# A macaron decoder block on one core: later work for the second half of a normalisation, and two overwritten 192-column products

## The chip, the cores and the metric

The kernel runs on one core of one Trainium2 chip. The metric is the device time of one execution in microseconds (us). Three runs of the kernel before took 958.99, 968.86 and 957.89 us; the median is 958.99 us. One further execution was recorded by the hardware profiler: it took 969.29 us, of which its instructions span 967.5 us.

## The reference

One decoder block on 512 tokens of width 1024: a SwiGLU feed-forward (hidden width 2816), a token mixer, a second SwiGLU feed-forward, each behind an RMSNorm with a learned shift and scale from a condition vector, and a last RMSNorm. All inputs are float32.

```python
cond = jax.nn.silu(c)
mod = cond @ w_ada[l] + b_ada[l]                      # nine vectors: shift, scale, gate, three times
u = modulate(rmsnorm(h, g_norm_ffn1[l]), sh1, sc1)
h = h + 0.5 * gt1 * swiglu(u, w_ffn1_in[l], w_ffn1_out[l])
u = modulate(rmsnorm(h, g_norm_mix[l]), sh2, sc2)
h = h + gt2 * token_mixing(u, cos, sin, ...)          # pooling and dilated attention, gated, then w_out
u = modulate(rmsnorm(h, g_norm_ffn2[l]), sh3, sc3)
h = h + 0.5 * gt3 * swiglu(u, w_ffn2_in[l], w_ffn2_out[l])
return rmsnorm(h, g_final)
def swiglu(u, w_in, w_out):
    a, b = jnp.split(u @ w_in, 2, axis=-1)
    return (jax.nn.silu(a) * b) @ w_out
```

## The kernel before, in words

**Data.** Features lie on the 128 partitions and the 512 tokens along the free axis, so the residual stream `H` is eight tiles of 128 x 512. To keep float32 accuracy every operand of a product is split in two parts, a rounded one and the rest: weights into `whi` and `wlo`, the normed input into `UH` and `UL`. One product then is three matmuls, high by high, high by low and low by high (`mm3`, lines 424 to 426; in the double pairs lines 794 to 796).

**Weights.** They come by DMA in chunks of 128 x 1024 into a few raw buffers. For each chunk ScalarE writes the rounded part (`split_hi`, line 377) and VectorE the rest (`split_lo`, line 389) into two rings, `whi` and `wlo`. The calls `look(n)` and `split(n)` in the code say how many chunks ahead of TensorE this is done. `self.half` holds a chunk whose high part is written and whose low part isn't. The order of the instructions on each engine is that in which the code calls them (a manual schedule), and each engine works through its own list; semaphores join them.

**Double pairs.** Most of the feed-forward is computed two hidden tiles at a time by a scheme of the Strassen kind, with seven products of 24 matmuls (128 x 256 each) where eight would be needed (`duo` and `product`). For that it uses sums of blocks of the input: `S[0]`, `S[1]` and `S[2]` in tiles `SH` and `SL`, made by `u_steps` (steps called `x22`, `x21`, `x11`, `x12` for the sums on VectorE, `s0`, `s1`, `s2`, `s3` for their two parts: `s0[0]` the high one on ScalarE, `s0[1]` the low one on VectorE, lines 757 and 758). The tile `X` holds four blocks, a11, a12, a21 and a22. Some of the sums of weight chunks are made on VectorE too (`X` <- raw, line 312). The output parts (`out_blocks`) use the same scheme on the hidden values.

**Around the change.** Only the way into the second feed-forward is touched. Its stages, with the times of the profiled execution:

- `out_tail` (to about 629 us) ends the mixer: the last three tiles of its output product for token half A (tokens 0 to 255), then for half B. For each tile, `tail_step` adds the product to `H` (line 600, VectorE) and squares it (line 601, ScalarE); the squares are summed into `AR` (line 651, VectorE). In half B's second tile, `stats_t` sums A's squares over the features (line 512), ScalarE takes the root (line 514), VectorE the reciprocal (line 517), and `spread` spreads it over the partitions on TensorE (line 522).
- `head` (about 629 to 650 us) computes the first two hidden pairs with whole products. In half A (loop value `h` 0) the normed input of B is begun: per tile, line 535 on VectorE, line 547 on ScalarE (`UH`), line 565 on VectorE (`UL`). Line 552 on ScalarE writes the unsplit input into `X`; for half A's upper four tiles that is put off in the list `self.rows`.
- `ffn2` then makes the sums, takes the SiLU of the first pairs (line 725) and goes into the first double pair (hidden tiles 2 and 3), at about 650 us, the second (tiles 4 and 5) and the first output part.

**Overwritten products.** `settle` (line 430) issues one matmul of 240 columns into a bank that the next product overwrites: `start=True` follows, so its result is never used. Before the change it stands at nine places in the trace, all of them ahead of 609 us.

Of the kernel before, what the change touches and what calls it, by code (L numbers as in the profile page):

```python
# [11 lines left out]
AF = mybir.ActivationFunctionType  # L12
# [4 lines left out]
HT = 256  # L17
# [121 lines left out]
SHIFT = 16  # L139

PLAIN = {0: 6, 2: 2}
# [24 lines left out]
class Kernel:  # L166
# [258 lines left out]
        M(ps, hi, ul, start=False, stop=False)  # L425
        M(ps, lo, uh, start=False, stop=stop)  # L426

    def settle(self, bank, hi, uh):

        self.nc.tensor.matmul(bank[:, :HT - SHIFT], hi, uh[:, SHIFT:HT], start=True, stop=True, skip_group_check=True)  # L430

    def nb(self):
        b = self.banks[self.bi % len(self.banks)]
# [163 lines left out]
    def tail_step(self, m, hs, bank, gate, s):  # L597

        Hm = self.H[m][:, hs]
        self.nc.vector.scalar_tensor_tensor(Hm, bank[:, hs], gate[:, m:m + 1], Hm, op0=OP.mult, op1=OP.add)  # L600
        self.nc.scalar.activation(s, Hm, AF.Square)

    def out_tail(self, ms, ksrc, gate, nxt, squares, beside=None):


        nc = self.nc
        tiles, starts, put, rest = {}, {}, [], self.spare()
        A, Bh = slice(0, HT), slice(HT, T)
        step = None
        self.held = self.pos  # L610
        for h, hs in enumerate((A, Bh)):
            for m in ms:
                bank = self.nb()
                if h == 0:
                    starts[m] = self.pos
                    tiles[m] = ksrc(m)
                    starts[m + 1] = self.pos
                if h == 0 and m == ms[0]:
                    nc.scalar.preload_act_table(AF.Sqrt)
                behind = h == 1 and m == ms[1]  # L620
                if self.done < self.pos + 4 and not behind:
                    self.split_hi()
                ks = tiles[m]
                if h == 0 and m == ms[0]:
                    self.settle(bank, ks[0][0], ks[0][2])
                for i, (hi, lo, uh, ul) in enumerate(ks):
                    if behind and i == len(ks) // 2:
                        self.stats_t(rest[0], A)
                        if self.done < self.pos + 4:
                            self.split_hi()  # L630
                        if self.half and len(self.half[1]) > 1:
                            self.split_lo(True)
                    if h == 1 and m == ms[2] and i == 0:
                        self.spread(rest[0], A)
                        step = self.norm_steps(nxt, A)
                        if nxt == 2:
                            step.three()
                        step(0)
                        self.split_lo()
                        self.fetch()  # L640
                    self.mm3(bank[:, hs], hi, lo, uh[:, hs], ul[:, hs], i == 0, i == len(ks) - 1)
                if step and m == ms[-1]:
                    step.low()
                    step.high()
                s = squares(m)[:, :HT]
                self.tail_step(m, hs, bank, gate, s)
                if h == 1:
                    self.held = starts[m + 1]
                    if step:
                        step(1 if m != ms[-1] else 3)  # L650
                put.append(lambda s=s, hs=hs: nc.vector.tensor_tensor(self.acc[:, hs], self.acc[:, hs], s, op=OP.add))
                do = lambda: [put.pop(0)() for _ in range(len(put))]
                if nxt == 2 and h == 0 and m == ms[-1]:
                    do()
                if not behind:
                    self.split_lo()
                    self.fetch()
                if beside and h == 0 and m == ms[0]:
                    beside()
                if h == 0 or m != ms[1]:  # L660
                    do()
        self.stepA = step

    def head(self, n, banks, table, between=(), beside={}):
# [9 lines left out]
        for h, hs in enumerate((A, Bh)):  # L674
            for i, (k, which) in enumerate(steps if h == 0 else [(k, both) for k in range(KT)]):
                if h == 0:
                    if i == 4:
                        self.stats_t(self.spare()[1], Bh)
                        nc.scalar.preload_act_table(table)
                    stepA(min(i, 5) + 2)  # L680
                    if i == 8:
                        self.spread(self.spare()[1], Bh)
                    if i > 7:
                        stepB(i - 8)
                        if n == 2 and i == 8:
                            stepB.low()
                            while self.rows:
                                self.rows.pop(0)()
                else:
                    stepB(k + 3)  # L690
                for f in beside.get((h, i), ()):
                    f()
                for j in which:
                    self.mm3(banks[j][:, hs], *w[j][k], self.UH[k][:, hs], self.UL[k][:, hs], k == 0, k == KT - 1)
                if (h, i) in ((0, 8), (1, 2), (1, 5)):
                    if h and between:
                        between.pop(0)()
                    if n == 2 and (h, i) == (1, 2):
                        stepB.high()
                        stepB.low()  # L700
                    self.split(self.done)
                    self.fetch()
        for f in between:
            f()
        self.held = None
# [79 lines left out]
    def product(self, bank, u, start, extra=0, other=None):  # L785
        M = self.nc.tensor.matmul
        w = self.take()
        if extra:
            self.settle(other if other is not None else bank, w[0][0], self.UH[0])
        for p in range(2):  # L790
            o = bank[:, p * HT:(p + 1) * HT]
            for k in range(4):
# [6 lines left out]
    def duo(self, n, j, first, last, extra):  # L799
# [33 lines left out]
        for i, (bank, u, start) in enumerate(((A, blk(lo4, T1), True), (B, S[0], True), (A, S[1], False),  # L833
# [10 lines left out]
                    f()  # L844
            elif not late:
                self.look(i if last and n and i > 4 else 2 if second and behind else 3 if early and i < 4 or behind or second else 4)
            w = self.product(bank, u, start, 0 if i else extra)
            if beside and i == 0:
                nc.tensor.matmul(C[:, :HT], w[0][0], u[0][0], start=False, stop=True, skip_group_check=True)
            self.step()  # L850
# [278 lines left out]
    def out_blocks(self, n, k0):  # L1129
# [72 lines left out]
    def ffn2(self):  # L1202
# [8 lines left out]
        for f in (x22, s0[0], x21):  # L1211
            f()
        h0, h1 = (self.ffn_silu(j, bk[2 * j]) for j in range(2))
        for f in (x11, s1[0], s0[1], s1[1]):
            f()
        late = self.block_hidden(0)
        two = lambda: self.look(2)
        b4, b5 = (self.banks[(self.bi + i) % 6] for i in range(2))

        def begin():  # L1220
            two()
            x12()
            s2[0]()
            self.free += self.rawx[1:]
# [1073 lines left out]
```

## Time and profile before

| | |
|---|---|
| median of 3 runs (each) | 958.99 us (958.99, 968.86, 957.89) |
| profiled execution, its span | 969.29 us, 967.5 us |
| TensorE matmuls, busy | 7352, 959.3 us (99%) |
| TensorE weight loads, busy | 907.7 us (94%) |
| VectorE busy | 842.2 us (87%) |
| ScalarE busy | 545.4 us (56%) |
| GpSimd busy | 90.5 us (9%) |
| granted TensorE clock | 0.999 |

Busy time is the union of an engine's instructions. Matmuls overlap in the record (each of 256 columns is shown with some 0.28 us while one starts every 0.113 to 0.118 us), so the start-to-start step of neighbouring matmuls says more than their duration. An instruction's idle time stands in brackets behind it in the timeline, with what ended it. A timeline row merges neighbours of one form and starts with the time from the span's start and the time that it covers.

### The profile page before, as it was taken

The numbers are of one execution on the slowest core, as the hardware profiler recorded it, in microseconds if no ns is written. First come the engines' busy times: TensorE is split into PE (matmuls) and PEld (weight loads), VectorE is DVE, ScalarE is ACT, GpSimd is POOL, SyncE is SP. The second block draws the span as 40 slices with busy tenths as digits, with TensorE's granted clock in tenths as the row PEclk, the third lists the DMA queues.
The fourth block names the chain that finished last, engine by engine and source line by source line (L and its number), as shares of the span: only waits on it lengthen the run. The fifth ranks groups of instructions, "written<-read, shape, count | busy, mean of one in ns | idle before, by whom it ended". The sixth has DMA issues, their size and how long they took to land.

```text
span 967.5 us, 18319 instructions
## 1 busy us (share of the span) xinstructions
PE 959.3 (99%) x7352; PEld 907.7 (94%) x7352; DVE 842.2 (87%) x1241; ACT 545.4 (56%) x829; POOL 90.5 (9%) x110
## 2 busy tenths in 40 slices
PE   9999999999999999999999999999999999999997
PEld 7888999999999999788899998999999999999997
DVE  7989999899998788886979768989998988879886
ACT  6453666665745453454565552477755656556555
POOL 0000100100010003007200000011011001000002
PEclk9999999999999999999999999999999999999999
DMA  9856776776868548857365446646766566665632
GB/s 357 283 191 240 209 218 166 207 207 152 223 170 246 174 153 254 260 189 197 77 186 158 137 144 224 206 102 185 200 166 161 140 173 164 166 153 140 163 81 88
DMA packets 55304, 176.81 MB, mean 183 GB/s; under 512 B 7857, under 2 KB 11569, under 8 KB 54962
## 3 DMA queue, kind: packets, MB, share of 16 engines
q1 hardware_dynamic: 44800, 141.82, 44.6%
q0 software_dynamic: 9840, 33.30, 19.2%
q8 instruction: 57, 0.93, 0.4%
q10 hardware_dynamic: 578, 0.53, 0.2%
q14 instruction: 29, 0.24, 0.1%
HBM read 135.36 MB, written 2.24 MB: 142 GB/s over the span
## 4 chain that ended last, share of the span: by engine, by line
PE 90%; DVE 4%; DMA 2%; ACT 1%; issue 1%; POOL 0%; SPq 0%; POOLq 0%; DVEq 0%; ACTq 0%
PE bank L795 15%; PE bank L794 15%; PE bank L796 15%; PE bank L424 6%; PE bank L425 6%; PE bank L426 6%; PE bank L1176 5%; PE bank L1175 5%; PE bank L1177 5%; PE bank L2219 2%; PE bank L2222 2%; PE bank L2224 1%; DVE wlo L389 1%; DMA v<-wada 1%; PE bank L1862 1%
## 5 line engine op out<-in xcount | busy, mean ns | idle before, releaser
L389 DVE TENSOR_TENSOR wlo<-raw,whi 128x1024 fp32r<-128x1024 f32 (+3 forms) x148 | 164.9, 1123 | 37.7 <-ACT whi L377 37.5
L794 PE MATMUL bank<-UH,whi 128*128 128x256 f32 x704 | 195.9, 278 | 0.0
L796 PE MATMUL bank<-UH,wlo 128*128 128x256 f32 x704 | 195.9, 278 | 0.0
L795 PE MATMUL bank<-UL,whi 128*128 128x256 f32 x704 | 195.9, 278 | 0.0
L389 DVE TENSOR_TENSOR wlo<-X,whi 128x1024 fp32r<-128x1024 f32 (+3 forms) x138 | 147.0, 1077 | 25.5 <-ACT whi L377 25.4
L377 ACT ACTIVATE whi<-raw 128x1024 fp32r<-128x1024 f32 (+3 forms) x148 | 141.3, 968 | 22.9 <-DMA raw<-wf1o 6.4
L377 ACT ACTIVATE whi<-X 128x1024 fp32r<-128x1024 f32 (+3 forms) x138 | 127.2, 942 | 42.9 <-DVE X L312 39.1
L794 PEld LDWEIGHTS bank<-UH,whi 128*128 128x128 f32 x704 | 133.5, 190 | 0.2
L795 PEld LDWEIGHTS bank<-UL,whi 128*128 128x128 f32 x704 | 132.2, 188 | 0.0
L796 PEld LDWEIGHTS bank<-UH,wlo 128*128 128x128 f32 x704 | 132.2, 188 | 0.0
L795 PE MATMUL bank<-SL,whi 128*128 128x256 f32 x432 | 120.5, 279 | 0.0
L796 PE MATMUL bank<-SH,wlo 128*128 128x256 f32 x432 | 120.4, 279 | 0.0
L794 PE MATMUL bank<-SH,whi 128*128 128x256 f32 x432 | 120.4, 279 | 0.0
L794 PEld LDWEIGHTS bank<-SH,whi 128*128 128x128 f32 x432 | 82.1, 190 | 0.0
L795 PEld LDWEIGHTS bank<-SL,whi 128*128 128x128 f32 x432 | 81.1, 188 | 0.2 <-DVE SL L758 0.2
L796 PEld LDWEIGHTS bank<-SH,wlo 128*128 128x128 f32 x432 | 81.1, 188 | 0.0
L424 PE MATMUL bank<-UH,whi 128*128 128x256 f32 (+1 forms) x240 | 80.4, 335 | 0.0
L425 PE MATMUL bank<-UL,whi 128*128 128x256 f32 (+1 forms) x240 | 79.2, 330 | 0.1
L426 PE MATMUL bank<-UH,wlo 128*128 128x256 f32 (+1 forms) x240 | 79.1, 330 | 0.0
L802 ACT ACTIVATE ev<-bank 128x512 f32<-128x512 f32 x54 | 32.1, 595 | 54.0 <-PE bank L796 53.8
L1175 PE MATMUL bank<-HI,whi 128*128 128x256 f32 x224 | 62.5, 279 | 0.0
L1176 PE MATMUL bank<-HK,whi 128*128 128x256 f32 x224 | 62.5, 279 | 0.0
(411 smaller groups left out, 2423.7 us busy)
## 6 DMA issues: line engine op xcount, KB each, us to landing
raw<-wmix SPq DMA_DIRECT2D x44, 512.0 KB, 4.2
raw<-wf1i SPq DMA_DIRECT2D x32, 512.0 KB, 5.7
raw<-wf2i SPq DMA_DIRECT2D x29, 512.0 KB, 4.5
ada<-wada SPq DMA_DIRECT2D x24, 512.0 KB, 6.0
X<-raw POOLq DMA_DIRECT2D x24, 512.0 KB, 5.2
xs<-wada SPq DMA_DIRECT2D x17, 512.0 KB, 6.0
X<-wf2i SPq DMA_DIRECT2D x15, 512.0 KB, 4.5
X<-wf1i SPq DMA_DIRECT2D x11, 512.0 KB, 4.3
```

Of the source, the lines that this page charges most:

```text
L377: self.nc.scalar.activation(self.hi[:, y], r[:, x], AF.Copy)
L389: self.nc.vector.tensor_tensor(self.lo[:, y], r[:, x], self.hi[:, y], op=OP.subtract)
L424: M(ps, hi, uh, start=start, stop=False)
L425: M(ps, hi, ul, start=False, stop=False)
L426: M(ps, lo, uh, start=False, stop=stop)
L794: M(o, hi, uh, start=start and p == 0 and k == 0, stop=False, skip_group_check=True)
L795: M(o, hi, ul, start=False, stop=False, skip_group_check=True)
L796: M(o, lo, uh, start=False, stop=k == 3, skip_group_check=True)
L802: copy = lambda o, x, f=1.0: nc.scalar.activation(o, x, AF.Copy, scale=f)
L1175: M(o, hi, uh, start=start and m % 2 == 0 and k == 0, stop=False, skip_group_check=True)
L1176: M(o, hi, ul, start=False, stop=False, skip_group_check=True)
L1177: M(o, lo, uh, start=False, stop=k == 1, skip_group_check=True)
```

## The change

1. In `out_tail`, the square of half B's first tile is issued later, behind the root of A's statistics; the sum of squares that uses it moves as well.
2. In `head`, the put-off rows (line 552, upper tiles of half A) are issued one split later, behind the high part of the next weight chunk; in half B, one split is opened up so that the last tile's `UL` stands ahead of the chunk's low part.
3. In `ffn2`, the low part of `S[0]` is issued ahead of the sum a11, the high part of the next weight chunk ahead of the high part of `S[1]`; a `look(2)` moves accordingly.
4. Two `settle` products of 192 columns are added: ahead of the second double pair of the second feed-forward, and ahead of its first output part. Each is one more weight load and one more matmul on TensorE (7050 rows become 7052).

```diff
-    def settle(self, bank, hi, uh):
+    def settle(self, bank, hi, uh, shift=SHIFT):
-        self.nc.tensor.matmul(bank[:, :HT - SHIFT], hi, uh[:, SHIFT:HT], start=True, stop=True, skip_group_check=True)
+        self.nc.tensor.matmul(bank[:, :HT - shift], hi, uh[:, shift:HT], start=True, stop=True, skip_group_check=True)
...
-        self.nc.scalar.activation(s, Hm, AF.Square)
+        return lambda: self.nc.scalar.activation(s, Hm, AF.Square)
...
                         self.stats_t(rest[0], A)
+                        while squared:
+                            squared.pop(0)()
                         if self.done < self.pos + 4:
                             self.split_hi()
                         if self.half and len(self.half[1]) > 1:
                             self.split_lo(True)
+                        do()
...
-                self.tail_step(m, hs, bank, gate, s)
+                square = self.tail_step(m, hs, bank, gate, s)
+                first = nxt == 2 and h == 1 and m == ms[0]
+                if first:
+                    squared.append(square)
+                else:
+                    square()
...
-                if h == 0 or m != ms[1]:
+                if h == 0 or m != ms[1] and not first:
                     do()
...
                             stepB.low()
-                            while self.rows:
-                                self.rows.pop(0)()
...
                         stepB.high()
                         stepB.low()
-                    self.split(self.done)
+                        self.split_lo()
+                        self.split_hi()
+                        stepB(6)
+                        stepB.low()
+                    self.split(self.done - bool(self.half))
                     self.fetch()
+                    while self.rows:
+                        self.rows.pop(0)()
...
-            self.settle(other if other is not None else bank, w[0][0], self.UH[0])
+            self.settle(other if other is not None else bank, w[0][0], self.UH[0], extra * SHIFT)
...
-            w = self.product(bank, u, start, 0 if i else extra)
+            w = self.product(bank, u, start, 0 if i else 4 if n and j == PLAIN[n] + 2 else extra)
...
             w, uk = self.take(), blk(u)
+            if n and k0 == 0 and i == 0:
+                self.settle(A[0], w[0][0], self.UH[0], 4 * SHIFT)
...
-        for f in (x11, s1[0], s0[1], s1[1]):
+        two = lambda: self.look(2)
+        for f in (s0[1], x11, two, s1[0], s1[1]):
             f()
         late = self.block_hidden(0)
-        two = lambda: self.look(2)
...
         def begin():
-            two()
             x12()
             s2[0]()
```

ScalarE at the end of the mixer's tail, half B: `gc` and `gs` are the buffers of the squares (line 601), `r_80` holds the root of A's statistics. Before:

```order
L601 ACTIVATE gs<-H 128x256
L377 ACTIVATE whi<-raw_64 128x1024
L601 ACTIVATE gc<-H 128x256 x2
L514 ACTIVATE r_80<-bank_96,eps 128x2
L377 ACTIVATE whi<-raw_65 128x512 x2
L601 ACTIVATE gs<-H 128x256
```

After:

```order
L601 ACTIVATE gs<-H 128x256
L377 ACTIVATE whi<-raw_64 128x1024
L601 ACTIVATE gc<-H 128x256
L514 ACTIVATE r_80<-bank_96,eps 128x2
L601 ACTIVATE gc<-H 128x256
L377 ACTIVATE whi<-raw_65 128x512 x2
L601 ACTIVATE gs<-H 128x256
```

The second of the two squares into `gc`, that of half B's first tile, now stands behind the root. On VectorE the reciprocal of the root moves with it, from behind the sum of that square to ahead of it.

ScalarE in `head`, at the turn from half A to half B: `UH<-ev,mod` is the high part of the normed input, `X<-ev,mod` the unsplit rows. Before:

```order
L679 ACT_TABLE_LOAD
L547 ACTIVATE UH<-ev,mod 128x256 x2
L552 ACTIVATE X<-ev,mod 128x256
L547 ACTIVATE UH<-ev,mod 128x256
L552 ACTIVATE X<-ev,mod 128x256 x4
L377 ACTIVATE whi<-raw_63 128x1024
L547 ACTIVATE UH<-ev,mod 128x256
```

After:

```order
L687 ACT_TABLE_LOAD
L547 ACTIVATE UH<-ev,mod 128x256 x2
L552 ACTIVATE X<-ev,mod 128x256
L547 ACTIVATE UH<-ev,mod 128x256
L552 ACTIVATE X<-ev,mod 128x256
L377 ACTIVATE whi<-raw_63 128x1024
L552 ACTIVATE X<-ev,mod 128x256 x3
L547 ACTIVATE UH<-ev,mod 128x256
```

Three of the four rows have moved behind the high part of the chunk `raw_63`, and ahead of the next `UH`.

VectorE between `head` and the first double pair: `X_6245` and `X_6246` are weight chunks, the plain `X` the blocks of the input, `SL_6251` and `SL_6253` the low parts of `S[0]` and `S[1]`. Before:

```order
L312 TENSOR_TENSOR X_6246<-raw_65,X_6245 128x1024
L389 TENSOR_TENSOR wlo<-X_6245,whi 128x1024
L565 SCALAR_TENSOR_TENSOR UL<-ev,mod,UH 128x256
L753 TENSOR_TENSOR X<-X 128x1024 x2
L762 SCALAR_TENSOR_TENSOR X<-X 128x1024
L758 TENSOR_TENSOR SL_6251<-X,SH_6250 128x1024
L758 TENSOR_TENSOR SL_6253<-X,SH_6252 128x1024
L389 TENSOR_TENSOR wlo<-X_6246,whi 128x1024
L762 SCALAR_TENSOR_TENSOR X<-X 128x1024
```

After:

```order
L312 TENSOR_TENSOR X_6246<-raw_65,X_6245 128x1024
L565 SCALAR_TENSOR_TENSOR UL<-ev,mod,UH 128x256
L389 TENSOR_TENSOR wlo<-X_6245,whi 128x1024
L765 TENSOR_TENSOR X<-X 128x1024 x2
L770 TENSOR_TENSOR SL_6251<-X,SH_6250 128x1024
L774 SCALAR_TENSOR_TENSOR X<-X 128x1024
L389 TENSOR_TENSOR wlo<-X_6246,whi 128x1024
L770 TENSOR_TENSOR SL_6253<-X,SH_6252 128x1024
L774 SCALAR_TENSOR_TENSOR X<-X 128x1024
```

`UL` of the last tile has moved ahead of a low part, `SL_6251` ahead of the sum a11, and the low part of `X_6246` ahead of `SL_6253`; on ScalarE the high part of `X_6246` has likewise moved ahead of the high part of `S[1]`. The DMA issues on SyncE and GpSimd keep their order.

More of the change, by code (lines that the diff above doesn't have):

```diff
@@ L600, in tail_step @@
         self.nc.vector.scalar_tensor_tensor(Hm, bank[:, hs], gate[:, m:m + 1], Hm, op0=OP.mult, op1=OP.add)
-        self.nc.scalar.activation(s, Hm, AF.Square)
+        return lambda: self.nc.scalar.activation(s, Hm, AF.Square)
     def out_tail(self, ms, ksrc, gate, nxt, squares, beside=None):
         nc = self.nc
-        tiles, starts, put, rest = {}, {}, [], self.spare()
+        tiles, starts, put, squared, rest = {}, {}, [], [], self.spare()
+        do = lambda: [put.pop(0)() for _ in range(len(put))]
         A, Bh = slice(0, HT), slice(HT, T)
@@ L651, in out_tail @@
                 put.append(lambda s=s, hs=hs: nc.vector.tensor_tensor(self.acc[:, hs], self.acc[:, hs], s, op=OP.add))
-                do = lambda: [put.pop(0)() for _ in range(len(put))]
                 if nxt == 2 and h == 0 and m == ms[-1]:
```

## The prediction

> **What bounds the kernel now.** I read the page first, then TensorE by stretches, then the waits in the stretch that the change touches. The page says that TensorE is never idle, and its clock was granted in full.
>
> ```profile
> span 967.5 us, 18319 instructions
> PE 959.3 (99%) x7352; PEld 907.7 (94%) x7352; DVE 842.2 (87%) x1241; ACT 545.4 (56%) x829; POOL 90.5 (9%) x110
> ...
> PEclk9999999999999999999999999999999999999999
> ```
>
> So whatever is to be won is won in the pace of TensorE, and busy time cannot show it: a waiting or slow matmul counts as busy. The view of stretches also counts the matmuls. The first row is from the first feed-forward, the second from the second one; both hold almost nothing but matmuls of 256 columns. The columns are the stretch, its length, then each engine's busy time and instructions.
>
> ```profile
> core 0: us, PE busy (x) PEld busy (x) DVE busy (x) ACT busy (x) POOL busy (x), PEclk, DMA share, GB/s
> 110.00:300.00 190.00, 190.00 (x1679) 190.00 (x1678) 180.06 (x235) 116.97 (x161) 17.22 (x20) 1.00 0.74 201
> 652.90:933.20 280.30, 280.30 (x2382) 280.30 (x2382) 248.53 (x302) 170.74 (x226) 24.16 (x28) 1.00 0.63 162
> ```
>
> An edge cuts matmuls of 0.28 us, so some 2.4 of each count lie across the edges: 190.00 / 1676.6 = 113.3 ns a matmul in the first, 280.30 / 2379.6 = 117.8 ns in the second, both at a clock of 1.00. The same instruction has **two paces**, 4.5 ns apart. The second one begins at a wait. The chain of waits shows it; its columns are start, share of time and what.
>
> ```profile
> 652.40 0.11 PE bank L849
> 652.52 0.11 PE bank L794
> 652.63 0.38 PE bank L795
> 653.01 0.12 PE bank L796
> ```
>
> Before the wait at 652.63 us the steps are 0.11 us, behind it 0.12 us, and by the row above it stays so on the mean to the end of that stretch. That is 2380 matmuls at 4.5 ns, **10.6 us**. Now the times of the runs fall into place: 957.89 and 958.99 us against 968.86 us and the profiled 969.29 us, 10.6 us apart on their means (958.4 and 969.1). I conclude, though the profile holds only one execution, that the kernel runs the second feed-forward at either pace, and that the median of 958.99 us is one of the quick kind.
>
> **The change, part by part.** Three waits of TensorE lie in the stretch. The first is ahead of the spread of A's statistics (line 522), which waits for a reciprocal on VectorE.
>
> ```profile
> 622.47 0.42 ACT L601 ACTIVATE gc<-H 128x256 f32<-128x256 f32 x1 [2.08 <-DVE H L600]
> 622.79 0.24 ACT L514 ACTIVATE r<-bank,eps 128x2 f32<-128x2 f32 x1
> ...
> 623.26 0.16 DVE L517 RECIPROCAL r<-r 128x2 f32<-128x2 f32 x1
> ...
> 623.08 0.28 PE L426 MATMUL bank<-v,wlo 128*128 128x256 f32 x1
> 623.48 0.43 PE L522 MATMUL bank<-cst,r 128*128 128x128 f32 x2
> ```
>
> The step from 623.08 to 623.48 us is 0.40 instead of 0.11, so 0.29 us are lost. ScalarE idled 2.08 us ahead of the square, with the root queued behind it. With the root in front, the reciprocal can follow as soon as VectorE is free of its step at line 600, which let the square start at 622.47; that is 0.8 us earlier than now, and the wait goes. The root then runs in that idle time and the square keeps its start; were the statistics late, the square would slip by the root's 0.24 us at most.
>
> The second wait is in half B's first tile. The chain runs back through ScalarE.
>
> ```profile
> 636.02 1.60 ACT X L552 x4
> 637.62 0.96 ACT whi L377
> 638.61 1.23 DVE wlo L389
> 639.84 0.40 DVE ev L535
> ...
> 640.26 0.51 ACT L547 ACTIVATE UH<-ev,mod 128x256 fp32r<-128x256 f32 x1 [1.68 <-DVE ev L535]
> ...
> 640.81 0.50 DVE UL L565
> ...
> 640.83 0.38 PE L424 MATMUL bank<-UH,whi 128*128 128x256 f32 x1
> 641.35 0.39 PE L425 MATMUL bank<-UL,whi 128*128 128x256 f32 x1
> 641.58 0.28 PE L426 MATMUL bank<-UH,wlo 128*128 128x256 f32 x1
> ```
>
> From 640.83 to 641.58 us two matmuls take 0.75 instead of 0.23 us: 0.52 us lost. Three of the four rows at 0.40 us each move behind `whi`, so `whi` ends 1.2 us earlier. VectorE, however, is held until 637.6 us by the sum before it.
>
> ```profile
> 636.46 1.22 DVE L312 TENSOR_TENSOR X<-raw,raw 128x1024 f32<-128x1024 f32 x1
> ...
> 647.69 2.48 DVE L753 TENSOR_TENSOR X<-X 128x1024 f32<-128x1024 f32 x2
> 650.21 1.22 DVE L762 SCALAR_TENSOR_TENSOR X<-X 128x1024 f32<-128x1024 f32 x1
> 651.35 2.44 DVE L758 TENSOR_TENSOR SL<-X,SH 128x1024 fp32r<-128x1024 f32 x2
> ...
> 652.62 0.19 PEld L795 LDWEIGHTS bank<-SL,whi 128*128 128x128 f32 x1 [0.19 <-DVE SL L758]
> ...
> 652.60 0.33 SPq L295 DMA_DIRECT2D X<-wf2i  x1
> ```
>
> So `wlo` starts at 637.6 instead of 638.61, the chain gains some 0.95 us, and `UL` is ready at 641.3 - 0.95 = 640.35. The matmul that reads it would be due one step behind 640.83, at 640.94, and 0.29 earlier with the first wait gone: 640.65. So the wait goes with 0.3 us to spare; if half of the gain fails, 0.2 us of it stay. The three rows move into ScalarE's idle time behind the chunk (the 1.68 us ahead of `UH`) and cost nothing there; their readers, the sums of line 753, start at 647.69.
>
> The third wait is the one that turns the pace: TensorE wants the low part of `S[0]` at about 652.5 us, and the first of the two of line 758 ends at 652.57. The chain's step of 0.38 instead of 0.11 us loses 0.27. The change takes the 1.14 us of a11 (line 762) out of the way, and the earlier `UL` and `head` chain give 0.4 and 0.95 us more: it is ready by about 650.1 us, while TensorE asks at 652.5 - 0.81 = 651.7. What could be late next is `SL` of `S[1]`: behind a11 and the `wlo` that now comes first it ends near 650.1 + 3 x 1.14 = 653.5 us, 0.3 us ahead of now, and TensorE asks 25 matmuls after the first, at 654.5. The DMA that refills a22 was issued at 652.60, when the first `SL` had read it; a11 now reads it last, at about 651.3, so it is no later.
>
> Two products of 192 columns are **added**. The trace has none, but it has the 240-column ones. In a running row of 256 it looks so:
>
> ```profile
> 367.51 0.28 PE L430 MATMUL bank<-whi,UH 128*128 128x240 f32 x1
> 367.63 0.28 PE L1778 MATMUL bank<-whi,UH 128*128 128x256 f32 x1
> ...
> 367.98 0.28 PE L1778 MATMUL bank<-whi,UH 128*128 128x256 f32 x1
> ...
> 482.86 0.38 PE L430 MATMUL bank<-UH,whi 128*128 128x240 f32 x1
> 483.08 0.28 PE L794 MATMUL bank<-k,whi 128*128 128x256 f32 x1
> ```
>
> At 367.51 us it and the three behind it take 0.47 us, three alone 0.34: 0.13 us. Behind a break, at 482.86, it takes 0.22. It is an extra instruction, so it costs no less than its columns, 192/256 of 113 ns = 0.085. I take 0.1 each, **0.2 us**; bounds 0.17 and 0.44. What it does to the pace can't be read from a 192 row; behind the 240-column one at 367.51 the three steps of 367.63 to 367.98 are 0.117 us on the mean, and I find no row in which one turns the pace.
>
> The sum against the profiled execution, which lies 1.8 us over its span: 969.29 - 10.6 (pace) - 0.29 - 0.52 - 0.27 (waits) + 0.2 = **957.8 us**. Against the two quick runs, which have the 10.6 already: 958.4 - 1.1 + 0.2 = 957.5. I predict **957.7 us**: within 0.2% of the median, since that was quick. What the change is worth is in the run that does not become 969.
>
> **A rule that speaks against it.** The Trainium skill, in "TensorE: Matmul & The Clock Gate", section "Step-by-step: what each phase is for", says that TensorE reads the moving operand and the weights by two independent ports, so that loading the next weights takes nothing from the running matmul; its section "Back-to-back issue gap" gives 256/2.4 + 2.5 = 109 ns (an estimate by that page). By that there is one pace and nothing for a short product to set right: an estimate of 969.3 - 1.1 + 0.2 = 968.4 where the run was slow. "Perfetto Trace Analysis", section "Identifying the Most-Contended Engine", tells to read headroom from the weight loads' busy share. The rows above show them at 190.00 of 190.00 and at 280.30 of 280.30 us, with 4% between the paces, so here neither rule holds.
>
> **The rivals.**
>
> *VectorE falls behind* (6%). At the slow pace it was full through the first two double pairs:
>
> ```profile
> 652.90:671.00 18.10, 18.10 (x156) 18.10 (x156) 17.83 (x20) 13.21 (x16) 1.71 (x2) 1.00 0.71 199
> 671.00:690.00 19.00, 19.00 (x164) 19.00 (x163) 18.83 (x22) 13.94 (x19) 2.37 (x3) 1.00 0.77 199
> ...
> 676.06 2.35 DVE L389 TENSOR_TENSOR wlo<-raw,whi 128x1024 fp32r<-128x1024 f32 x2
> ...
> 678.29 0.28 PE L796 MATMUL bank<-UH,wlo 128*128 128x256 f32 x1
> ```
>
> The first `wlo` of the third row ends at 677.28, its first reader starts at 678.29: 1.0 us of margin. At the quick pace TensorE gets there 9 products x 24 matmuls x 4.5 ns = 0.97 us earlier, and 1.08 us for the waits; VectorE has moved by some 1.3. That leaves 0.3 us. If VectorE's gain is lost, 1.0 us comes back as a wait: 958.7. Against it: the quick runs of before met nearly the same margin and show no such loss.
>
> *The added product turns the quick pace into the slow one* (8%), the other side: slower than before. A wait of 0.27 us did that at 652.63; a product of 64 columns less shifts the row of loads and streams too. Place: the second double pair, at 671 us. Price: the matmuls from there on, 2380 less the 156 of the row up to 671, at 4.5 ns, 10 us: 957.7 + 10 = 967.7 us, 0.9% over the median. It decides if most runs turn. Against it: the 240-column ones did not.
>
> *It doesn't do what it says* (6%): a short product leaves the pace as it is and some wait left over still draws it anew in each execution, as two of the four before were slow; the runs then lie at 957.7 and 957.7 + 10.6 = 968.3, and the median on either. Against it: the wait that turned the pace at 652.63 is taken away. The Trainium skill's rule of two ports, above, would end here.
>
> **How the numbers follow.** The forecast has 80%: 957.7, and 956.3 to 959.5 by the bounds above (0.24 us on the products, 0.3 on the second wait, 1.1 us between the two quick runs). The range 956.3 to 960.3 takes in VectorE's case and half of the last, and leaves out the slow pace. A change is told from none at 2%, that is 19 us, and no case reaches so far: faster 1%, same 98%, slower 1%.
>
> **What would show it.** Right: no step of 0.27 us or more at the spread, at half B's first tile and at the first `SL`; steps of 0.113 us from there on, and as many matmuls per us in the second feed-forward as between 110 and 300 us. Wrong: 0.118 us behind a 192-column product, or waits of TensorE for line 389 between 655 and 690 us.

## The result, and the profile after

The changed kernel takes **958.2 us** (median of 22 runs, 957.45 to 959.89). The kernel before, run beside it, takes 968.87 us (median of 22, 957.89 to 970.07): its executions lie on two levels, 10 of them at 957.89 to 959.42 and 12 at 968.86 to 970.07. All 22 of the changed kernel lie on the lower one. The ratio, worked out over all runs and not from the two medians, is 0.9938, with a 95% interval of 0.9912 to 0.9965. So the time is near the one that I predicted, 957.7 us, but the kernel is 0.6% faster than the one before, and by the medians 1.1%, where I had forecast no change. The profiled execution after took 958.99 us.

The page of the changed kernel, the span and the busy times:

```profile
span 957.2 us, 18324 instructions
PE 948.1 (99%) x7354; PEld 897.4 (94%) x7354; DVE 842.1 (88%) x1241; ACT 545.8 (57%) x829; POOL 90.5 (9%) x110
```

TensorE has 7354 matmuls, two more than before, and a span 10.3 us shorter, at the same 99%: as before, busy time shows nothing. The view of stretches does. Its columns are the stretch, its length, then each engine's busy time and, in brackets, instructions; the count behind TensorE's is what to read. First the changed kernel:

```profile
core 0: us, PE busy (x) PEld busy (x) DVE busy (x) ACT busy (x) POOL busy (x), PEclk, DMA share, GB/s
110.00:300.00 190.00, 190.00 (x1679) 190.00 (x1678) 180.84 (x236) 116.81 (x162) 17.22 (x20) 1.00 0.74 201
...
700.00:915.00 215.00, 215.00 (x1899) 215.00 (x1898) 193.19 (x237) 131.47 (x174) 18.99 (x22) 1.00 0.64 165
```

The same 215 us of the kernel before hold 71 matmuls fewer:

```profile
700.00:915.00 215.00, 215.00 (x1828) 215.00 (x1827) 187.46 (x231) 125.01 (x166) 18.99 (x22) 1.00 0.63 159
```

With 2.4 of each count across the edges that is 113.4 ns a matmul after and 117.8 before, both at a clock of 1.00. The first feed-forward has 1679 matmuls in 190 us in both kernels. I call the two paces quick (113 ns) and slow (118 ns).

**The three waits.** TensorE's rows in the changed kernel at the spread, at half B's first tile and at the first `SL` (start, duration, instruction):

```profile
623.82 0.28 PE L426 MATMUL bank<-v,wlo 128*128 128x256 f32 x1
623.94 0.38 PE L522 MATMUL bank<-cst,r 128*128 128x128 f32 x2
...
641.08 0.28 PE L424 MATMUL bank<-UH,whi 128*128 128x256 f32 x1
641.20 0.28 PE L425 MATMUL bank<-UL,whi 128*128 128x256 f32 x1
...
652.76 0.28 PE L806 MATMUL bank<-SH,whi 128*128 128x256 f32 x1
652.87 0.28 PE L807 MATMUL bank<-SL,whi 128*128 128x256 f32 x1
652.98 0.28 PE L808 MATMUL bank<-SH,wlo 128*128 128x256 f32 x1
```

All steps are 0.11 to 0.12 us: the three waits are gone. But there is a new one, in half B's tail:

```profile
626.92 0.28 PE L424 MATMUL bank<-UH,whi 128*128 128x256 f32 x1
627.21 0.39 PE L425 MATMUL bank<-UL,whi 128*128 128x256 f32 x1
627.43 0.28 PE L426 MATMUL bank<-UH,wlo 128*128 128x256 f32 x1
```

From 626.92 to 627.43 us two steps take 0.51 instead of 0.23: 0.28 us lost, all of what the spread had won. At 629.43 us another 0.07 us go. VectorE's and ScalarE's rows show why:

```profile
622.74 0.26 ACT L514 ACTIVATE r<-bank,eps 128x2 f32<-128x2 f32 x1 [1.64 <-PE bank L512]
623.19 0.42 ACT L601 ACTIVATE gc<-H 128x256 f32<-128x256 f32 x1 [0.18 <-DVE H L600]
...
624.16 0.69 DVE L389 TENSOR_TENSOR wlo<-raw,whi 128x512 fp32r<-128x512 f32 x1 [0.96 <-ACT whi L377]
624.77 0.42 DVE L660 TENSOR_TENSOR AR<-AR,gc 128x256 f32<-128x256 f32 x1
...
626.67 0.48 DVE L565 SCALAR_TENSOR_TENSOR UL<-ev,mod,UH 128x256 fp32r<-128x256 f32 x1
```

The square stands behind the root, and its sum into `AR` now stands behind the chunk's first low part, ahead of the steps that lead to `UL`. VectorE idles 0.96 us ahead of that low part, in which the sum could have run, and is busy without a break behind it. `UL` is due earlier, since TensorE is, and comes later by the 0.34 us from 624.77 to the next start.

These waits differ from execution to execution. Of the kept profiles, 13 have the old order in the tail: seven of them show no wait at the spread, the other six lose 0.08 to 0.55 us there, and the mean of all is 0.16 us. Five have the tail as changed: one, the one above, loses 0.35 us near 627 and 629 us, four lose 0.11 us at 628 to 629 us, and the mean is 0.16 us again.

**The products.** One of the two, in the changed kernel's row:

```profile
668.96 0.28 PE L808 MATMUL bank<-UH,wlo 128*128 128x256 f32 x1
669.08 0.25 PE L430 MATMUL bank<-UH,whi 128*128 128x192 f32 x1
669.16 0.30 PE L806 MATMUL bank<-UH,whi 128*128 128x256 f32 x1
669.30 0.28 PE L807 MATMUL bank<-UL,whi 128*128 128x256 f32 x1
```

From 668.96 to 669.30 us three steps take 0.34, as three plain ones do. So it costs one plain step, 0.113 us, for its 192 columns, and the row goes on at the quick pace.

### The profile page after: what moved, and what is told of

It is laid out like the page before. It is cut to its first block, busy times and chain, and to the rows that moved or that the text cites. A ratio compares the mean times of both kernels' runs of the same rounds, so it can differ in the third digit from the quotient of the medians.

```text
span 957.2 us, 18324 instructions
## 1 busy us (share of the span) xinstructions
PE 948.1 (99%) x7354; PEld 897.4 (94%) x7354; DVE 842.1 (88%) x1241; ACT 545.8 (57%) x829; POOL 90.5 (9%) x110
## 4 chain that ended last, share of the span: by engine, by line
PE 97%; DMA 1%; issue 1%; POOL 0%; DVE 0%; ACT 0%; SPq 0%; POOLq 0%
PE bank L806 15%; PE bank L808 15%; PE bank L807 15%; PE bank L424 9%; PE bank L425 9%; PE bank L426 9%; PE bank L1191 5%; PE bank L1189 5%; PE bank L1190 5%; PE bank L2232 2%; PE bank L2235 2%; PE bank L2237 2%; PE bank L1566 1%; PE bank L1617 1%; PE bank L1875 1%; PE bank L1876 1%
## 5 line engine op out<-in xcount | busy, mean ns | idle before, releaser
L1191 PE MATMUL bank<-HI,wlo 128*128 128x256 f32 x224 | 61.8, 276 | 0.0
```

Of the source, the lines that this page charges most:

```text
L1191: M(o, lo, uh, start=False, stop=k == 1, skip_group_check=True)
```

## Experiments

The question was which part makes the kernel steadily quick. My theory was that it is the wait at the first `SL`; the rivals were the wait at half B's first tile, and the two products, which might set a slow row right. Shares of quick runs are counted with all runs of one kernel, and the ratio, over all runs as above, is against the kernel before in the same comparison.

### The new order without the products (order_only)

```diff
-            w = self.product(bank, u, start, 0 if i else 4 if n and j == PLAIN[n] + 2 else extra)
+            w = self.product(bank, u, start, 0 if i else extra)
...
-            if n and k0 == 0 and i == 0:
-                self.settle(A[0], w[0][0], self.UH[0], 4 * SHIFT)
```

> The changed kernel without its two products of 192 columns: the new order alone. Theory P (the pace of the second feed-forward is drawn at the 0.27 us wait for the low part of S[0]; the new order takes that wait away): every run is a quick one, 958.4 us less the 0.23 us of the two products, so 957.7 to 958.8, no run near 969; steps of 0.113 us from 650 us on in the profile. Theory R (the products are what holds the quick pace): runs at 958 and at 969 us mixed, as in the kernel before (12 of 22 slow). Theory B (both are needed): also mixed, but with fewer at 969.

Eleven of 12 runs are quick (mean 958.42 us), one took 968.65; median 958.51, ratio 0.9948 (0.9908 to 0.9988). The order by itself does nearly all of it.

### The products in the old order (products_only)

```diff
+            w = self.product(bank, u, start, 0 if i else 4 if n and j == PLAIN[n] + 2 else extra)
...
+            if n and k0 == 0 and i == 0:
+                self.settle(A[0], w[0][0], self.UH[0], 4 * SHIFT)
```

> The kernel before with the two products of 192 columns and nothing else; the 0.27 us wait stays. Theory P (in the changed kernel's profile the step of the product and the next matmul are 86 and 141 ns, together two plain steps, so it shifts nothing): mixed runs, at 958.9 and 969.5 us. Theory R (the product sets the slow pace right): all runs at 958.9 to 959.7 us, since only the 156 matmuls between the wait and the first product stay slow, 156 x 4.5 ns = 0.7 us; the profile then shows 0.118 us steps only up to about 671 us.

Twelve of 12 are quick, 958.13 to 960.63 us, median 959.14, ratio 0.9943 (0.9907 to 0.9980). The order of the rest is the old one, so the products do it another way. In the profile the wait at half B's first tile is there; at the first `SL` there is none, as TensorE comes there later:

```profile
641.02 0.35 PE L424 MATMUL bank<-UH,whi 128*128 128x256 f32 x1
641.51 0.39 PE L425 MATMUL bank<-UL,whi 128*128 128x256 f32 x1
641.73 0.28 PE L426 MATMUL bank<-UH,wlo 128*128 128x256 f32 x1
...
652.92 0.28 PE L794 MATMUL bank<-SH,whi 128*128 128x256 f32 x1
653.03 0.28 PE L795 MATMUL bank<-SL,whi 128*128 128x256 f32 x1
```

The 71 steps from 632.96 to 641.02 us are 113.5 ns on the mean, the 95 from 641.73 to 652.92 us are 117.8. So the row turned slow at the wait near 641 us, 11 us ahead of the one that I had blamed. TensorE's rows around the first product:

```profile
669.76 0.28 PE L796 MATMUL bank<-UH,wlo 128*128 128x256 f32 x1
669.88 0.25 PE L430 MATMUL bank<-UH,whi 128*128 128x192 f32 x1
669.97 0.30 PE L794 MATMUL bank<-UH,whi 128*128 128x256 f32 x1
```

and the stretches ahead of and behind it:

```profile
652.90:668.50 15.60, 15.60 (x135) 15.60 (x134) 15.53 (x18) 12.22 (x15) 1.71 (x2) 1.00 0.70 201
672.00:686.00 14.00, 14.00 (x126) 14.00 (x126) 13.83 (x18) 10.59 (x15) 1.75 (x2) 1.00 0.70 195
```

15.60 / 132.6 = 117.6 ns ahead, 14.00 / 123.6 = 113.3 behind. The row came in slow and left quick: the 192-column product set it right.

### Part 3 alone (low_first)

```diff
-        for f in (x11, s1[0], s0[1], s1[1]):
+        two = lambda: self.look(2)
+        for f in (s0[1], x11, two, s1[0], s1[1]):
...
```

> The kernel before with part 3 of the change alone: the low part of S[0] ahead of a11, and the high part of the next weight chunk ahead of that of S[1]. Theory P: the wait at 652.6 us is gone (a11's 1.14 us is more than 0.27), the waits of 0.29 and 0.52 us at 623 and 641 us stay, and all runs are quick: 958.6 - 0.3 = 958.3 us. Rival Q (any of the three waits draws the pace): mixed, at 958.3 and 969 us.

Two of 12 quick, ten at 968.94 to 969.68; median 969.14, ratio 1.0022 (0.9983 to 1.0061). The wait at the first `SL` is gone in its profile, which is of a quick run, and the kernel is no better for it. My theory fell. What is left there is a short wait of 0.08 us near 655 us and the one at half B's first tile:

```profile
641.02 0.28 PE L424 MATMUL bank<-UH,whi 128*128 128x256 f32 x1
641.30 0.39 PE L425 MATMUL bank<-UL,whi 128*128 128x256 f32 x1
641.53 0.28 PE L426 MATMUL bank<-UH,wlo 128*128 128x256 f32 x1
```

### Products of 240 columns (products_240)

```diff
+            w = self.product(bank, u, start, 0 if i else 1 if n and j == PLAIN[n] + 2 else extra)
...
+                self.settle(A[0], w[0][0], self.UH[0], SHIFT)
```

> The kernel before with the two added products at 240 columns instead of 192. Theory P for the width: 240 columns shift the row of steps (0.111, 0.124, 0.116 and 0.115 us behind the one at 367.5 us, against 0.086 and 0.141 for 192), so the pace behind it may be another one than ahead of it: all runs on one side, at 959.5 us if it sets the slow pace right, at 968.5 to 969.5 if it makes it slow. Rival: it shifts nothing here, and runs are mixed at 958.9 and 969.5 us.

Ten of 12 at 959.29 to 961.28 us (mean 959.99), two at 968.35 and 968.78; ratio 0.9964 (0.9923 to 1.0005). In its profile the row came in quick, and the 240-column product turned it slow; the first and the last of the plain steps on each side:

```profile
668.49 0.28 PE L794 MATMUL bank<-UH,whi 128*128 128x256 f32 x1
668.61 0.28 PE L795 MATMUL bank<-UL,whi 128*128 128x256 f32 x1
668.72 0.28 PE L796 MATMUL bank<-UH,wlo 128*128 128x256 f32 x1
668.83 0.27 PE L430 MATMUL bank<-UH,whi 128*128 128x240 f32 x1
668.94 0.28 PE L794 MATMUL bank<-UH,whi 128*128 128x256 f32 x1
...
669.88 0.28 PE L796 MATMUL bank<-UH,wlo 128*128 128x256 f32 x1
```

Behind it 668.94 to 669.88 us are 8 steps of 0.118; up to the second product the row stays slow, behind that one, at 688.7 us, it is quick. So in this execution 240 columns turned the pace, in both directions. If they did so each time, the rows that come in slow, about half, would also leave slow; that is two of 12 runs here.

### Part 2 alone (head_only), and parts 2 and 3 (head_and_low)

```diff
-                            while self.rows:
-                                self.rows.pop(0)()
...
-                    self.split(self.done)
+                        self.split_lo()
+                        self.split_hi()
+                        stepB(6)
+                        stepB.low()
+                    self.split(self.done - bool(self.half))
                     self.fetch()
+                    while self.rows:
+                        self.rows.pop(0)()
```

> The kernel before with part 2 of the change alone: the three rows of the upper tiles behind the chunk's high part. The runs so far: with part 3 alone (no wait at the first SL) 10 of 12 were slow, so that wait is not what draws the pace by itself. Theory Q (each wait inside the rows of 256-column products draws the pace anew): the 0.52 us wait near 641 us goes, that of 0.27 at the first SL stays or grows, since TensorE comes earlier; runs mixed at 958.2 and 968.8 us. Rival U (the wait near 641 us alone draws it): all runs quick, 958.2 us.

> Parts 2 and 3 of the change, without part 1 and without the added products. Theory Q: no wait is left between 631 us and the end of the second feed-forward, so nearly all runs are quick, as with the whole new order (11 of 12), and at its time, 958.4 us or 0.1 less: part 1 wins 0.29 us at the spread and loses 0.35 us near 627 us in the changed kernel's profile. If part 1 is worth its 0.29 us, 958.8 us.

Both are quick in 12 of 12 runs: part 2 alone has a median of 958.46 us, ratio 0.9938 (0.9902 to 0.9974), both parts 958.09, ratio 0.9935 (0.9897 to 0.9972). Part 2 takes the wait at 641 us away, as expected; that the 0.27 us at the first `SL` would stay was wrong. VectorE's and TensorE's rows of part 2 alone:

```profile
650.95 2.44 DVE L762 TENSOR_TENSOR SL<-X,SH 128x1024 fp32r<-128x1024 f32 x2
...
652.84 0.28 PE L798 MATMUL bank<-SH,whi 128*128 128x256 f32 x1
652.95 0.28 PE L799 MATMUL bank<-SL,whi 128*128 128x256 f32 x1
```

The first of the two low parts ends near 652.17, some 0.8 us ahead of its reader. So part 2 by itself removes both waits that can draw the pace; part 3 adds margin. Its two moves, the three rows and the last tile's `UL`, were not run apart.

### One product alone in the old order (one_product, product_late)

The first has only the line in `product` of products_only, ahead of the second double pair, the second only that ahead of the output part.

> The kernel before with only the first of the two added products, ahead of the second double pair. If one product of 192 columns sets the slow pace right for good (no wait behind it), all runs are quick at 959.1 us, 0.11 less than with both (959.14 median) or equal within the noise. If the second is needed, some runs are at 969.

> The kernel before with only the second of the two added products, ahead of the first output part. If a wait between about 670 and 689 us draws the pace anew and none later, all runs are quick at 958.8 to 960.3 us (up to 330 matmuls x 4.5 ns = 1.5 us of slow pace from 652 to 689 us, where it was drawn slow). If the product fails on a slow pace drawn by a wait, about a third of half the runs are at 969.

Each is quick in 8 of 12 runs (958.38 to 959.92 and 958.65 to 960.55 us) and slow in 4 (968.83 to 970.47 and 969.84 to 971.29); ratios 0.9977 (0.9932 to 1.0022) and 1.0004 (0.9956 to 1.0051). If a 192-column product always set a slow row right, all 12 would be quick for the first. To see one that fails, three more executions of the first kernel and two of the second were profiled:

> One look at one_product (before with the first product alone). If the execution is slow (one in three): theory W (a later wait) has 0.113 us steps behind the product at about 670 us and 0.118 from a wait between there and 690 us on; theory F (the product fails) has 0.118 on both sides of it. If it is quick: 959.3 us.

> A second look at one_product: slow (near 970 us) in one of three, and then 0.118 us steps from a later wait on by theory W, on both sides of the product by theory F; else 959.3 us.

> A third look at one_product: slow (near 970 us) in one of three, and then 0.118 us steps from a later wait on by theory W, on both sides of the product by theory F; else 959.3 us.

> One look at product_late (before with the second product alone): slow (near 970 us) in one of three. Then theory F (the product fails on some slow paces) has 0.118 us steps on both sides of it, theory W (drawn anew later) 0.113 behind it and 0.118 from a later wait on. If quick: 959 to 960.5 us.

> A second look at product_late: slow (near 970 us) in one of three. Then theory F has 0.118 us steps on both sides of the product, theory W 0.113 behind it and 0.118 from a later wait on. If quick: 959 to 960.5 us.

All five were quick (959.11, 959.55, 959.31, 958.82 and 958.39 us), so what goes wrong in the other third was not seen. One of the first kernel's, one_product_c, shows a row that came in slow and left quick, ahead of the product and behind it:

```profile
654.50:668.50 14.00, 14.00 (x121) 14.00 (x121) 13.93 (x17) 10.62 (x13) 1.71 (x2) 1.00 0.70 209
...
700.00:915.00 215.00, 215.00 (x1899) 215.00 (x1899) 193.36 (x237) 131.32 (x175) 19.00 (x22) 1.00 0.64 166
```

That is 14.00 / 118.6 = 118.0 ns ahead and 113.4 behind.

### A row made slow, and set right (made_slow, made_slow_then_192)

The new order without its products; the first kernel adds one 240-column product ahead of the first double pair, the second also the 192-column one ahead of the second.

```diff
+            w = self.product(bank, u, start, 0 if i else 1 if n and j == PLAIN[n] else extra)
...
+            w = self.product(bank, u, start, 0 if i else 1 if n and j == PLAIN[n] else 4 if n and j == PLAIN[n] + 2 else extra)
```

> The new order without the two products of 192 columns, and one product of 240 columns ahead of the first double pair, where the pace is quick. If a 240-column product turns the pace, as it did at 668.6 us (quick to slow) and at 688.5 us (back) in the run with two of them, all runs are slow: some 2400 matmuls x 4.5 ns = 10.8 us over the 958.4 of the new order, 969.2 us. Rival (it turned it there by chance): 958.5 us, or mixed.

> As made_slow, with one product of 192 columns ahead of the second double pair. If 192 columns set the slow pace right each time, all runs are at 958.4 + 168 matmuls x 4.5 ns + 0.2 = 959.4 us. With the kernel before and this one product 4 of 12 runs stayed near 970; if that was the product failing to set the pace right, about a third or more of these runs are at 969; if it was a later wait, none are, because the new order has no later wait.

The first is slow in 10 of 10 runs, median 969.03 us, 968.41 to 969.96; the second quick in 7 of 7, median 959.63, 958.86 to 960.55. In the profile of the first the pace is slow to the end:

```profile
700.00:915.00 215.00, 215.00 (x1828) 215.00 (x1827) 187.24 (x231) 125.00 (x166) 18.99 (x22) 1.00 0.62 159
```

In that of the second it is slow up to the 192-column product and quick behind it; the stretches on each side:

```profile
652.90:668.50 15.60, 15.60 (x134) 15.60 (x134) 15.41 (x18) 11.54 (x14) 1.71 (x2) 1.00 0.71 205
672.00:686.00 14.00, 14.00 (x126) 14.00 (x125) 12.93 (x17) 10.18 (x15) 1.75 (x2) 1.00 0.64 170
```

One overwritten product of 0.1 us so costs 10.5 us (969.03 against 958.51 without it), and another gives 9.4 of it back. All other instructions stand in the same order in both and in the kernel without them, so this shows most plainly that the two levels of time are the two paces.

### The sum ahead of the low part (sum_ahead), and both again

A try at a better version: the sum of the square stands ahead of the chunk's first low part, in VectorE's idle 0.96 us, and only the first product is kept.

```diff
                             self.split_hi()
+                        do()
                         if self.half and len(self.half[1]) > 1:
                             self.split_lo(True)
-                        do()
```

> The changed kernel, the sum of half B's first square issued ahead of the chunk's first low part instead of behind it, and only the first of the two products. VectorE sat idle for 0.96 us ahead of that low part (until 624.16 us in the changed kernel's profile), and the square was there at 623.6, so the sum of 0.34 us fits in; the low parts of half A's first tile then come 0.34 us earlier and the waits of 0.35 us near 627 us go. All runs quick: 958.4 - 0.35 - 0.11 = 957.9 us. If the wait stays, 958.3.

> The kernel sum_ahead once more, beside the changed one on the same chip: 0.35 us of waits near 627 us and 0.11 us of one product less, so 0.3 to 0.5 us below changed_again, if the waits were worth what the profile shows; equal within 0.2 us otherwise.

> The changed kernel once more, to stand beside sum_ahead on one chip: 958.2 to 958.6 us, all quick.

It is quick in 12 of 12 runs, median 958.19 us, and again in 5 of 5, median 958.38, beside 958.25 of the changed kernel (5 of 5, 957.51 to 958.58). In its first profile no wait is left between 625 and 631 us; in its second 0.11 us are lost at 628.9 us, as much as in four of the five profiles of the tail as changed. So that the sum's place costs TensorE 0.28 us is shown for one execution alone. A gain over the changed kernel can't be measured.

## Why the prediction was right and wrong

**The step that failed** is the conclusion "the median of 958.99 us is one of the quick kind", from which "within 0.2% of the median, since that was quick" followed. The two paces, the 10.6 us between them and the place where they part in that execution were read rightly, but a median of three executions was taken as the kernel's usual time. In all comparisons together the kernel before was quick in 61 of 127 executions (10 of 22, 16 of 35, 18 of 35, 7 of 17, 10 of 17 and 0 of 1). With four times in hand, two of each kind, the record had said as much: half of the executions lose 10.6 us, so a change that takes the cause away is worth some 5.5 us on the mean, and from nothing to 11 us on a median. That the median of the three was a quick one was chance; in the five larger comparisons it is 968.87, 968.94, 960.06, 968.83 and 959.67 us. I had the sentence, "what the change is worth is in the run that does not become 969", and gave its worth no chance of showing.

**The pace, 10.6 us:** right in size. The made_slow kernel puts 10.5 us on it.

**Who draws it:** that the third wait, at the first `SL`, "is the one that turns the pace" was incomplete. Taken away alone it left 2 of 12 runs quick; with the wait at half B's first tile taken away as well, 12 of 12 are. I had read the pace between 641 and 652 us in one execution only, in which it happened to be quick. The kept profiles show that each of the two waits can turn it, and that neither always does: of 11 rows with the wait near 641 us one left it slow (products_only), of nine with the wait at the first `SL` two did (before and one_product_c).

**The waits:** 0.29, 0.52 and 0.27 us went, as worked out, but they are those of one execution: 0.29 us at the spread is 0.16 on the mean of 13. That the moved square "keeps its start" was so (0.57 us behind the start of line 600 in both profiles), but its sum on VectorE was costed at nothing. Part 1 gives nothing net, neither in the profile after (0.35 us lost near 627 and 629 us) nor on the means.

**The products:** 0.1 us each was right, 0.113 measured. The 240-column row at 367.51 us, which seemed to say that such products are neutral, was read rightly and still misled. The three steps behind it are 0.117 us on the mean, but the row then goes on at the quick pace:

```profile
367.98 0.28 PE L1778 MATMUL bank<-whi,UH 128*128 128x256 f32 x1
...
371.95 0.28 PE L1780 MATMUL bank<-whi,UL 128*128 128x256 f32 x1
```

These are 35 steps of 113.4 ns. So 240 columns left this quick row as it was, and turned one at 649.49 us (made_slow) and at 668.83 us (products_240). The operands are named the other way round there (`whi,UH` against `UH,whi`); whether that is the reason, no run here shows.

**The sum** against the profiled execution gave 957.8 us; the runs' mean is 958.4. Quick against quick the forecast was a gain of 0.9 us. With the terms as the two profiles show them it is 0.52 + 0.27 + 0.29 - 0.35 - 0.23 = 0.50 us; the means give 0.25 in the first comparison (958.63 against 958.38, standard error some 0.2) and 0.87 in the later one (959.03 against 958.16, some 0.26), so no term is told apart by them.

**The rivals.** VectorE did not fall behind; its low parts at the second double pair have more margin than the 0.3 us that I worked out:

```profile
675.32 2.36 DVE L389 TENSOR_TENSOR wlo<-raw,whi 128x1024 fp32r<-128x1024 f32 x2
...
677.58 0.28 PE L808 MATMUL bank<-UH,wlo 128*128 128x256 f32 x1
```

The first of the two ends near 676.5, 1.0 us ahead of its reader. That the added product turns the quick pace into the slow one did not happen with 192 columns, and did with 240 in the second feed-forward: the mechanism was real, with another size. That the pace is drawn anew is what remains in one of the 12 runs of order_only. With the products it is none of 27, and without them none of the 24 runs of part 2 with or without part 3, so these runs don't show that the products help where part 2 is in.

**The rules of the Trainium skill.** "TensorE: Matmul & The Clock Gate", section "Step-by-step: what each phase is for", says that loading the next weights takes no read bandwidth from the running matmul; the prediction drew from it that there is one pace and nothing for a short product to set right. The runs decide against that conclusion: the two kernels with a row made slow differ by one such product, and by 9.4 us. What part the ports have in the slow pace they don't show. The prediction's 109 ns by the Trainium skill is, in the section "Back-to-back issue gap", the figure for a single matmul by itself; in a stream of pairs, it says, weight load and matmul both set the spacing. Here 113.3 and 117.8 ns were measured. And "Perfetto Trace Analysis" of the Trainium skill names the useful work per time ahead of the weight loads' share, and that is what the count per stretch measures.

**What stays open.** Why one 192-column product left 4 of 12 runs slow in the old order, where two left none of 12 and a row made slow by a 240-column product was set right in 7 of 7: no slow execution of it was profiled. The weight loads give a lead. In every long slow row kept of the second feed-forward, one load of the three of a product step is shown with 192 ns on the mean and the others with 188. It is the first of the three in the kernel before and the third in made_slow (both from 700 to 915 us), and the second in one_product_c (654 to 668 us); behind the bar stand the busy time in us and the mean of one load in ns:

```profile
L794 PEld LDWEIGHTS bank<-UH,whi 128*128 128x128 f32 x232 | 44.5, 192 | 0.0
...
L808 PEld LDWEIGHTS bank<-UH,wlo 128*128 128x128 f32 x232 | 44.5, 192 | 0.0
...
L795 PEld LDWEIGHTS bank<-UL,whi 128*128 128x128 f32 x20 | 3.8, 192 | 0.0
```

In the quick rows all three have 188. So there are three kinds of slow row. Those that a 192-column product is seen to set right have the long load third (products_only, made_slow_then_192) or second (one_product_c). Whether it fails where the long load is the first is not shown.

It is open, too, what in a wait decides the pace behind it. Its length, as recorded, doesn't: at the first `SL` a step of 0.27 us left the row slow in the kernel before and one_product_c and quick in products_240, and near 641 us one of 0.49 us left it slow in products_only and quick in one_product_c. And two of the 127 executions of the kernel before, at 964.85 and 965.50 us, lie between the levels, as if slow for 55 to 60% of the row (an estimate from the 10.6 us); they were not profiled.

## What to carry to other kernels

Where a long row of equal matmuls runs without a break, compare the count of instructions per stretch between stages and runs, not busy time: 4% hid in a TensorE that was 99% busy at full clock in both kernels. If times lie on two levels, ask how often each occurs before saying what a change is worth; a median of three can't tell. And take away every wait ahead of such a row, even one of 0.3 us, since what follows can cost 35 times as much; when an instruction is moved, price its followers on the other engines too.

## What the runs showed of the hardware

I had not expected that the same row of 256-column matmuls has two stable paces at a granted clock of 1.00, 113.3 and 117.8 ns, that a row can keep the one it has over some 280 us, and that a single overwritten matmul can change it. In the second feed-forward 240 columns turned quick to slow and slow to quick, and 192 turned slow to quick and left quick as it was; at 367.51 us 240 columns left a quick row quick. The weight loads are busy through the whole stretch at both paces (215.00 of 215.00 us), and differ in one load of three: 192 ns in the slow rows, 188 in the quick ones.
